# The adaLN product, the first load of x, the last store and the bias tables of the dilated heads rewritten

## The chip, the cores and the metric

One core of one Trainium2 chip runs the whole program. The metric is the device time of one execution in microseconds (us), as the median of several runs. Engines are written PE (matmul), PEld (weight load), DVE, ACT, POOL and SP; a "q" behind a name is the engine's DMA queue.

## What is computed

Two stacks of two layers over x of 256 rows and 1024 columns, all in fp32. A layer of the first stack is: SwiGLU feed-forward, a mixer of sliding-window attention and retention, a second feed-forward, each followed by a residual and a layer norm. A layer of the second stack is one mixer whose heads include six dilated heads, modulated by adaLN. What the change touches:

```python
def swiglu_ffn(x, w_gu, w_down):
    a, u = jnp.split(x @ w_gu, 2, axis=-1)
    return (jax.nn.silu(a) * u) @ w_down
...
# adaLN of a layer of the second stack: shift, scale and gate, 1024 each
mod = silu(c) @ w_ada + b_ada
# score bias of dilated head h between positions at distance dist
bias = log(count(dist)) - 2.0 ** (-8.0 * (h + 1) / 10.0) * dist
```

The bias's count says in how many of the dilation patterns (every key up to 128 back, every fourth, every sixteenth) a pair stands; pairs in none are masked.

## The kernel before, in words

**Weights.** All weights come in the order of one host-made list (`plan`) as pieces of up to 128 x 1024 fp32 (512 KB), loaded by SP's queue into `st`, a pool of 6 slots (NS). A product in fp32 is made of three: ACT rounds a piece to `whi` (line 300), DVE subtracts to get `wlo` (line 302), and PE multiplies hi by hi, hi by lo and lo by hi (`mm`, line 331). A slot is free again when DVE has read it, so an SP load waits, in order, for the DVE six slots back.

**Feed-forward.** `gu_T` (from line 520) makes one chunk of 128 gate and 128 up columns, transposed. For each of 8 steps k and two column halves it issues a pair of matmuls: one with `whi` against 512 columns (x hi and x lo side by side), one with `wlo` against 256. So a chunk has 16 pairs. There are 22 chunks; the down product `ac<-x..,h..` runs 6 chunks behind.

**Start.** The first feed-forward needs x transposed. `load_xT` (line 231) loads it in four quarters of 256 KB on SP's queue, each into one of the same six `st` slots, and splits it into `xx` (lines 377 and 378); the first chunk's weights come in pieces of 128, 128, 256, 256 and 256 KB (FIRST_K) between the quarters, the second chunk's as two of 512 KB. 18 bf16 matmuls on zeros go ahead on PE.

**adaLN.** `w_ada_2` is spread over the feed-forwards as pieces of 128 rows by 1024 columns, 48 in all (2 layers, 3 outputs, 8 row blocks). `ada_step` (line 306) multiplies each by its 128 values of silu(c) and adds it to `ada` on DVE (line 317, line 315 for the first of eight). After the eighth, eight transposes on PE (line 446) in two groups and two reductions on DVE (line 324) sum `ada` over the partitions into a column of `mod`. This happens six times, so 12 groups of four transposes.

**Dilated heads.** In each layer of the second stack, `score` makes the six dilated heads' scores in six banks: 384, 384, 512, 512, 256 and 256 columns. Line 660 adds the bias from `al`, which has two halves used in turn; line 1165 fills a half per bank, one DVE instruction per head, from `dist` and `lc` (log of the count). Then line 665 takes the row maximum, line 671 (ACT) the exponential, line 678 the reciprocal, line 1114 (ACT) the scaling, PE transposes P, and `PT` is copied by line 692 (ACT) or 694 (DVE) for the product with v (`ac<-PT,v..`). Beside it, ACT makes `sg` (line 1270), ahead of which its function table is loaded.

**Store.** The last layer norm writes each half of 128 rows in two scalings (line 422) and two stores on SP's queue (line 424).

The order of each engine's work is the order in which the code issues it, but for `issue_after`, which puts DVE and ACT work behind a named instruction.

Of the kernel before, what the change touches and what calls it, by code (L numbers as in the profile page):

```python
# [17 lines left out]
D = 1024  # L18
# [8 lines left out]
FIRST_K = ((0, 1), (1, 1), (2, 2), (4, 2), (6, 2))  # L27
# [31 lines left out]

G1 = in1_groups()  # L60
# [3 lines left out]
def plan(take):  # L64

    def piece(kind, name, l, k0, kk, cols):
        return kind, kk, len(cols), take(name, l, k0, kk, cols)

    def ffn(i, l):
        start = (i, l) == (1, 0)
        c0 = 0 if start else 4
        na = 0
        for c in range(0, c0, 2):
            cols = rng(128 * c, 256) + rng(DFF + 128 * c, 256)
            for k in (0, 2, 4, 6):
                yield piece("w", f"ffn{i}_w_gu", l, k, 2, cols)
        for c in range(c0, NCH):
            cols = rng(128 * c, 128) + rng(DFF + 128 * c, 128)  # L80
            for k, kk in FIRST_K if start and c == 0 else ((0, 4), (4, 4)):
                yield piece("w", f"ffn{i}_w_gu", l, k, kk, cols)
            if c >= NCH - 8 * len(ADA[i, l]):
                u, k = divmod(na, 8)
                al, q = ADA[i, l][u]
                yield piece("a", "w_ada_2", al, k, 1, rng(1024 * q, 1024))
# [12 lines left out]
    def outp(name, l):  # L99
        for k in range(8):  # L100
            yield piece("w", name, l, k, 1, rng(0, D))

    for l in range(DEPTH):
        yield from ffn(1, l)
        yield from groups("w_in", l, G1)
        yield from outp("w_out", l)
        yield from ffn(2, l)
    for l in range(DEPTH):
        yield from groups("w_in_2", l, G2[:5])
        for j in range(2):  # L110
            for k in (0, 3):
                yield piece("w", "w_uq_2", l, k, 3, rng(288 * j, 288))
        for k in range(2):
            yield piece("w", "w_ukv", l, k, 1, rng(0, 768))
        yield from groups("w_in_2", l, G2[5:])
        yield from outp("w_out_2", l)


def lay_out(inp):
    d = {}  # L120
    f = lambda a: np.ascontiguousarray(a)
    src = {**inp, "w_ukv": np.concatenate([inp["w_uk_2"], inp["w_uv_2"]], 2), "w_out_2": inp["w_out_2"][:, Y2]}
# [7 lines left out]
    d["xT"] = f(inp["x"][0].T.reshape(4, 2, 128, 2, 128).transpose(0, 2, 3, 1, 4).reshape(4, 128, 512))  # L130
    d["bada"] = f(inp["b_ada_2"].reshape(DEPTH * 24, 128).T)
    d["c"] = f(inp["c_2"].reshape(8, 128).T)
# [10 lines left out]
def tables():  # L143
# [31 lines left out]
    t["lc"] = lc.astype(f32)  # L175
    t["dist"] = dist.astype(f32)
    return {k: np.ascontiguousarray(v) for k, v in t.items()}
# [5 lines left out]
class Kernel:  # L183
# [12 lines left out]
    def setup(self):  # L196
# [9 lines left out]
        self.c = self.const.tile([128, 8], F32, name="c")  # L206
        self.sc = self.const.tile([128, 8], F32, name="sc")
        self.mod = [self.const.tile([128, 24], F32, name=f"mod{l}") for l in range(DEPTH)]
        nc.gpsimd.dma_start(out=self.idn, in_=d["idn"])
# [4 lines left out]
        nc.scalar.activation(out=self.sc, in_=self.mhalf, func=AF.Silu)  # L214
        self.xx = self.xt.tile([128, 2, 2, 8, 128], F32R, name="xx")
        self.xh, self.xl = self.xx[:, 0], self.xx[:, 1]
        self.xhl = self.xx.rearrange("p e t k n -> p (e t) k n")
        self.xT, self.yT = {}, {}
        self.n_ox = 0
        self.warm()  # L220
# [10 lines left out]
    def load_xT(self, q):  # L231

        st = self.stage.tile([128, 1024], F32, name="st")[:, :512]
        self.nc.sync.dma_start(out=st, in_=self.d["xT"][q])
        ks = slice(2 * q, 2 * q + 2)
        self.hilo(self.xh[:, :, ks, :], self.xl[:, :, ks, :], st.rearrange("p (t k n) -> p t k n", t=2, k=2))

    def load_x(self, c):

        if c == 7:  # L240
            for t in range(2):
                self.xT[t] = self.xh[:, t], self.xl[:, t]
                self.nc.sync.dma_start(out=self.x[t], in_=self.d["x"][128 * t:128 * t + 128, :])
            self.bada = self.const.tile([128, 48], F32, name="bada")
            self.nc.sync.dma_start(out=self.bada, in_=self.d["bada"])
            self.nc.sync.dma_start(out=self.c, in_=self.d["c"])
            self.nc.scalar.activation(out=self.sc, in_=self.c, func=AF.Silu)
# [6 lines left out]
    def open_block1(self):  # L254
# [5 lines left out]
        self.dec = p.tile([128, 2048], F32, name="dec")  # L260

# [3 lines left out]
    def open_block2(self):  # L265
# [6 lines left out]
        self.lc = p.tile([128, 384], F32, name="lc")  # L272
        for n in ("rt2", "cau", "dist", "lc"):
            nc.gpsimd.dma_start(out=getattr(self, n), in_=d[n])
# [31 lines left out]
    def ada_step(self, pool):  # L306

        nc = self.nc
        while self.pieces and self.pieces[0][0] == "a":
            _, l, k, _, cols = self.pieces[0][3]  # L310
            st = self.load_piece()[1]
            c = self.sc[:, k:k + 1]
# [5 lines left out]
            if k < 7:  # L318
                continue
            q = cols[0] // 1024  # L320
# [79 lines left out]
    def ln(self, t, banks, alpha, eps, gate=None):  # L400
# [16 lines left out]
        if self.at_end:  # L417
# [3 lines left out]
            for c0, c1 in HALVES:  # L421
                nc.vector.scalar_tensor_tensor(out=x[:, c0:c1], in0=x[:, c0:c1], scalar=y, in1=self.b[:, c0:c1],  # L422
                                               op0=ALU.mult, op1=ALU.add)
                nc.sync.dma_start(out=self.out[128 * t:128 * t + 128, c0:c1], in_=x[:, c0:c1])
# [50 lines left out]
class Ffn:  # L475
# [44 lines left out]
    def gu_T(self, c, pcs):  # L520
# [7 lines left out]
        for hi, lo, kk, _ in pcs:  # L528
            for i in range(kk):
                for j in range(2):  # L530
                    cs = slice(128 * j, 128 * j + 128)
                    o = ps[j].rearrange("p (a n) -> p a n", a=4)
                    K.mm(o, lhsT=hi[:, i, cs], rhs=K.xhl[:, :, k, :], start=k == 0, stop=False, skip_group_check=True)
                    K.mm(o[:, 0:2, :], lhsT=lo[:, i, cs], rhs=K.xh[:, :, k, :], start=False, stop=k == 7,
# [28 lines left out]
    def body(self):  # L563
        K = self.K
        if self.start:
            pcs = []
            for q in range(4):
                K.load_xT(q)
                pcs += K.get(1 if q else 2)
            self.gu_T(0, pcs)  # L570
        last = K.split
        for c in range(1 if self.start else 4, NCH):
            self.gu_T(c, K.get(2))
            if c in (7, 13, 15) and self.start:
                K.load_x(c)
            with K.tc.issue_after(last):
                K.ada_step(self.fp)
# [367 lines left out]
class Mixer2(OutProj, Attn):  # L945
# [223 lines left out]

    def body(self):  # L1170
# [128 lines left out]
        b_score, b_av = self.make(6, 0.125, half(qbT), keys(kbT), vb, 5, self.alibi(0, lambda t: self.seg(K.lc, t)), True)  # L1299
# [98 lines left out]
```

## Time and profile before

| | |
|---|---|
| median of 3 runs | 1345.4 us (1343.68, 1345.4, 1346.33) |
| the profiled execution | 1350.96 us, its span 1349.2 us |
| mean granted clock of TensorE | 0.994 |
| PE busy | 1319.8 us, 98% of the span |
| DVE busy / ACT busy / POOL busy | 76% / 55% / 2% |
| mean DMA rate | 195 GB/s |

The span is the time from the first to the last record; 1.8 us of the execution lie around it. In a timeline row the numbers are start and duration, both in us, then the engine, line, operation, output and inputs, shapes and count. A bracket at the end gives the idle time of the engine just before and what ended it. Matmuls overlap, so a matmul's duration is longer than the step from one to the next.

### The profile page before, as it was taken

How to read it: one execution, taken by the hardware profiler on the slowest of the kernel's cores; microseconds unless marked ns; L12 is line 12 of the kernel's file. 1: busy time of each engine (PE TensorE's matmuls, PEld its weight loads, DVE VectorE, ACT ScalarE, POOL GpSimd, SP SyncE). 2: the span in 40 equal slices, each digit the busy share in tenths (PEclk: the TensorE clock that was granted, in tenths of full speed). 3: DMA queues.
4: the chain of work that ended last, by engine and by line, in shares of the span. 5: the costliest groups of instructions: out<-in, count | busy, mean ns of one | idle time of the engine just before them, and what ended most of it. 6: DMA issues, size and time to landing. Idle time of an engine off the chain costs nothing. (4 is left out here: it accounts for less than half of the span.)

```text
span 1349.2 us, 20437 instructions
## 1 busy us (share of the span) xinstructions
PE 1319.8 (98%) x7654; PEld 1135.5 (84%) x7654; DVE 1031.4 (76%) x1713; ACT 741.4 (55%) x1310; POOL 25.8 (2%) x35
## 2 busy tenths in 40 slices
PE   8999999999999999999999999999999999999997
PEld 6888888788887888888887878888889998799886
DVE  6876769968977669787579878687585797866976
ACT  6654536446655546545446456555355678456681
POOL 0000000010000000000000110000000000000000
PEclk9999999999999999999999999999999999999999
DMA  8987724546878628877423637677445433464420
GB/s 290 332 297 234 240 93 133 203 134 232 316 244 268 212 83 305 299 255 250 156 96 125 252 124 269 202 260 265 131 151 184 154 126 128 138 203 160 143 77 32
DMA packets 75235, 262.88 MB, mean 195 GB/s; under 512 B 9168, under 2 KB 9552, under 8 KB 75008
## 3 DMA queue, kind: packets, MB, share of 16 engines
q1 hardware_dynamic: 74592, 259.82, 56.9%
q0 software_dynamic: 544, 1.75, 0.4%
q8 instruction: 60, 0.98, 0.3%
q14 instruction: 39, 0.32, 0.1%
HBM read 260.49 MB, written 1.05 MB: 194 GB/s over the span
## 5 line engine op out<-in xcount | busy, mean ns | idle before, releaser
L302 DVE TENSOR_TENSOR wlo<-st,whi 128x1024 fp32r<-128x1024 f32 (+4 forms) x319 | 372.3, 1176 | 74.6 <-ACT whi L300 73.1
L300 ACT ACTIVATE whi<-st 128x1024 fp32r<-128x1024 f32 (+4 forms) x319 | 322.6, 1021 | 123.4 <-PE mm L331 49.6
L331 PE MATMUL mm<-xx,whi 128*128 128x256 f32 (+1 forms) x1296 | 335.0, 334 | 1.2 <-DVE xx L378 1.2
L331 PE MATMUL mm<-xx,wlo 128*128 128x256 f32 x928 | 262.1, 283 | 0.0
L331 PEld LDWEIGHTS mm<-xx,whi 128*128 128x128 f32 x1296 | 221.0, 191 | 25.7 <-ACT whi L300 1.5
L331 PE MATMUL mm<-whi,xx 128*128 128x512 f32 (+3 forms) x744 | 219.1, 372 | 0.6 <-DVE xx L378 0.4
L331 PE MATMUL tr<-xx,whi 128*128 128x512 f32 x560 | 197.3, 394 | 2.2 <-ACT whi L300 2.2
L331 PEld LDWEIGHTS mm<-xx,wlo 128*128 128x128 f32 x928 | 176.8, 191 | 2.2 <-DVE wlo L302 0.5
L331 PE MATMUL tr<-xx,wlo 128*128 128x256 f32 x560 | 157.6, 282 | 0.5 <-DVE wlo L302 0.5
L331 PEld LDWEIGHTS mm<-whi,xx 128*128 128x128 f32 x744 | 135.0, 188 | 24.5 <-issue 1.6
L302 DVE TENSOR_TENSOR xlo<-st,xhi 128x1024 fp32r<-128x1024 f32 x106 | 128.4, 1219 | 26.0 <-ACT xhi L300 26.0
L300 ACT ACTIVATE xhi<-st 128x1024 fp32r<-128x1024 f32 x106 | 110.2, 1056 | 67.6 <-PE ac L331 56.3
L331 PE MATMUL mm<-wlo,xx 128*128 128x512 f32 (+3 forms) x372 | 137.0, 369 | 0.0
L331 PEld LDWEIGHTS tr<-xx,whi 128*128 128x128 f32 x560 | 105.4, 188 | 26.0 <-ACT whi L300 2.6
L331 PE MATMUL ac<-xlo,hth 128*128 128x512 f32 x320 | 126.2, 394 | 0.0
L331 PE MATMUL ac<-xhi,hth 128*128 128x512 f32 x320 | 125.4, 392 | 0.0
L331 PEld LDWEIGHTS tr<-xx,wlo 128*128 128x128 f32 x560 | 106.5, 190 | 2.2 <-DVE wlo L302 1.0
L331 PE MATMUL ac<-xhi,htl 128*128 128x512 f32 x320 | 105.0, 392 | 0.0
L317 DVE SCALAR_TENSOR_TENSOR ada<-st,sc,ada 128x1024 f32<-128x1024 f32 x42 | 53.8, 1281 | 41.5 <-DMA st<-in_w 41.5
L331 PEld LDWEIGHTS mm<-wlo,xx 128*128 128x128 f32 x372 | 70.1, 188 | 10.6 <-issue 0.3
L331 PEld LDWEIGHTS ac<-xhi,hth 128*128 128x128 f32 x320 | 60.1, 188 | 14.1
L331 PEld LDWEIGHTS ac<-xhi,htl 128*128 128x128 f32 x320 | 60.0, 188 | 12.4
(275 smaller groups left out, 1823.1 us busy)
## 6 DMA issues: line engine op xcount, KB each, us to landing
st<-in_w SPq DMA_DIRECT2D x442, 512.0 KB, 4.6
st<-in_w SPq DMA_DIRECT2D x20, 384.0 KB, 3.7
g<-in_lng SPq DMA_DIRECT2D x8, 512.0 KB, 4.8
b<-in_lnb SPq DMA_DIRECT2D x8, 512.0 KB, 5.2
st<-in_w SPq DMA_DIRECT2D x8, 432.0 KB, 4.1
st<-in_w SPq DMA_DIRECT2D x8, 296.0 KB, 3.9
st<-in_xT SPq DMA_DIRECT2D x4, 256.0 KB, 4.5
x<-in_x SPq DMA_DIRECT2D x2, 512.0 KB, 7.7
```

The source lines that it names most:

```text
L300: nc.scalar.activation(out=hi[:, :m], in_=st[:, :m], func=AF.Copy)
L302: nc.vector.tensor_tensor(out=lo[:, :m], in0=st[:, :m], in1=hi[:, :m].bitcast(F32), op=ALU.subtract)
L317: nc.vector.scalar_tensor_tensor(out=self.ada, in0=st, scalar=c, in1=self.ada, op0=ALU.mult, op1=ALU.add)
L331: return self.nc.tensor.matmul(*a, **k).ins
```

## The change

Four edits.

1. `w_ada_2` is transposed on the host, so a piece holds 128 output columns against all 1024 inputs. silu(c) is loaded onto all 128 partitions (512 KB, one ACT instruction of 128 x 1024). Each of the 48 pieces takes one DVE instruction that multiplies and sums along the row into its column of `mod`. The transposes and reductions are gone.
2. x's quarters are loaded into tiles that are idle at the start (`x[1]`, half of `x[0]`, `tmp`) and not into `st`; the first quarter comes as two DMAs on ACT's queue. `xx` has hi and lo of one k side by side. The second chunk's weights come as 256, 256 and 512 KB. `idn` and c are loaded later, at chunk 7.
3. The last store of 512 columns is split in 384 (ACT's queue) and 128.
4. The dilated heads' biases are made on the host, and each bank's half of `al` is loaded by POOL's queue. `lc` is not loaded.

```diff
-FIRST_K = ((0, 1), (1, 1), (2, 2), (4, 2), (6, 2))
+FIRST_K = (((0, 1), (1, 1), (2, 2), (4, 2), (6, 2)), ((0, 2), (2, 2), (4, 4)))
...
-        nc.scalar.activation(out=self.sc, in_=self.mhalf, func=AF.Silu)
...
+        self.xk = self.xt.tile([128, 8, 512], F32R, name="xx")
+        self.xh, self.xl = (self.xk[:, :, c:c + 256].rearrange("p k (t n) -> p t k n", t=2) for c in (0, 256))
...
+        self.xw = self.tmp()
+        for k in range(2):
+            nc.scalar.dma_start(out=self.x[1][:, 256 * k:256 * k + 256], in_=d["xT"][0][:, 256 * k:256 * k + 256])
+        nc.scalar.activation(out=self.one, in_=self.mhalf, func=AF.Silu)
...
+    def load_xT(self, k, n):
+        q, r = divmod(k, 2)
+        src = (self.x[1][:, 0:512], self.x[1][:, 512:], self.x[0][:, 512:], self.xw)[q][:, 256 * r:256 * (r + n)]
+        if q > 0:
+            self.nc.sync.dma_start(out=src, in_=self.d["xT"][q])
+        self.hilo(self.xk[:, k:k + n, :256], self.xk[:, k:k + n, 256:], src.rearrange("p (k n) -> p k n", k=n))
...
-            if k == 0:
-                self.ada = pool.tile([128, 1024], F32, tag="ada", name="ada", bufs=2)
-                nc.vector.tensor_scalar(out=self.ada, in0=st, scalar1=c, scalar2=None, op0=ALU.mult)
-            else:
-                nc.vector.scalar_tensor_tensor(out=self.ada, in0=st, scalar=c, in1=self.ada, op0=ALU.mult, op1=ALU.add)
...
+            nc.vector.scalar_tensor_tensor(out=st, in0=st, scalar=1.0, in1=self.sc, op0=ALU.mult, op1=ALU.mult,
+                                           accum_out=self.mod[l][:, j:j + 1])
...
-            for h in range(2):
-                ps = self.transposes([self.ada[:, 512 * h + 128 * i:512 * h + 128 * i + 128] for i in range(4)])
-                nc.vector.tensor_reduce(out=m[:, 4 * h:4 * h + 4], in_=ps.rearrange("p (k n) -> p k n", k=4), axis=AX.X,
-                                        op=ALU.add)
...
-            for c0, c1 in HALVES:
+            for c0, c1, q in ((0, 512, nc.sync), (512, 896, nc.scalar), (896, 1024, nc.sync)):
...
+    def alibi_b(self, t, hs, nk):
+        self.n_al += 1
+        w = self.al[:, self.n_al % 2, :len(hs) * nk]
+        self.K.nc.gpsimd.dma_start(out=w, in_=self.K.d[f"al{B_BANKS.index((nk, tuple(hs)))}"])
+        return w.rearrange("p (h n) -> p h n", h=len(hs))
...
-        b_score, b_av = self.make(6, 0.125, half(qbT), keys(kbT), vb, 5, self.alibi(0, lambda t: self.seg(K.lc, t)), True)
+        b_score, b_av = self.make(6, 0.125, half(qbT), keys(kbT), vb, 5, self.alibi_b, True)
```

**Order at the start, SP's queue.** Before, with what each load waits for (`st<-in_xT` is a quarter of x, `st<-in_w` a piece of weights; DVE is the slot's last reader):

```order
L234 DMA st<-in_xT 128x512
L284 DMA st<-in_w 128x256 x2
L234 DMA st<-in_xT 128x512
L284 DMA st<-in_w 128x512
L234 DMA st<-in_xT 128x512
L284 DMA st<-in_w 128x512 [waits DMAHW0_49,DVE_49]
L234 DMA st<-in_xT 128x512 [waits DMAHW1_49,DVE_49]
L284 DMA st<-in_w 128x512 [waits DMAHW2_49,DVE_49]
L284 DMA st<-in_w 128x1024 [waits DMAHW3_49,DVE_49]
L284 DMA st<-in_w 128x1024 [waits DMAHW4_49,DVE_49]
```

And now (`x_80`, `x_79` and `tmp` are the idle tiles):

```order
L290 DMA st<-in_w 128x256 x2
L240 DMA x_80<-in_xT 128x512
L290 DMA st<-in_w 128x512
L240 DMA x_79<-in_xT 128x512
L290 DMA st<-in_w 128x512
L240 DMA tmp<-in_xT 128x512 [waits DMAHW0_49]
L290 DMA st<-in_w 128x512 [waits DMAHW1_49]
L290 DMA st<-in_w 128x512 [waits DMAHW2_49]
L290 DMA st<-in_w 128x512 [waits DMAHW3_49,DVE_49]
L290 DMA st<-in_w 128x1024 [waits DMAHW4_49,DVE_49]
```

The first load that waits for DVE is now the tenth, the second piece of chunk 1; it was the seventh, and chunk 1's first piece stood behind four such waits.

**Order around a group of transposes on PE.** Before, at the end of a feed-forward (`hth` and `htl` are the chunk's hidden values):

```order
L331 MATMUL ac<-xhi,hth 128x512
L446 MATMUL tr<-idn,ada 128x128 x4
L331 MATMUL ac<-xlo,hth 128x512
L331 MATMUL ac<-xhi,htl 128x512 x2
L331 MATMUL ac<-xhi,hth 128x512
L446 MATMUL tr<-idn,ada 128x128 x4
L331 MATMUL ac<-xlo,hth 128x512
```

In the changed kernel the two rows of transposes are gone and nothing stands in their place; the rows around them are the same.

**Order at the first two banks of the dilated heads on DVE.** Now, with the waits (`P<-ac,al` is line 660 before; DMASW is a load of POOL's queue):

```order
L657 SCALAR_TENSOR_TENSOR P<-ac,al 128x512 [waits DVE_49,PE_49] x2
L662 TENSOR_REDUCE nm<-P 128x2 [waits DVE_49] x2
L308 TENSOR_TENSOR kkw<-st,qiTw 128x1024 [waits DMAHW7_49,Activation_49]
L675 RECIPROCAL rd<-den 128x2 [waits Activation_49]
L657 SCALAR_TENSOR_TENSOR P<-ac,al 128x384 [waits DMASW4_49,PE_49]
L675 RECIPROCAL rd<-den 128x2 [waits Activation_49]
L657 SCALAR_TENSOR_TENSOR P<-ac,al 128x384 [waits DMASW5_49,PE_49]
L662 TENSOR_REDUCE nm<-P 128x3 [waits DVE_49] x2
L691 COPY PT<-tr 128x512 [waits PE_49]
```

On POOL, the loads that these wait for:

```order
L1171 DMA al<-in_al 128x384 x2
L1171 DMA al<-in_al 128x512 x2
L1171 DMA al<-in_al 128x256 x2
```

Before, DVE's `al<-dist,lc` stood where `kkw` stands, and again between the banks; each load on POOL waits until DVE has read the same half two banks earlier.

## Rows read from the trace of the kernel before

**Rows 1.** The page's section 1: busy us, share of the span, instructions.

```profile
PE 1319.8 (98%) x7654; PEld 1135.5 (84%) x7654; DVE 1031.4 (76%) x1713; ACT 741.4 (55%) x1310; POOL 25.8 (2%) x35
```

**Rows 2.** The waits of PE: us in total, times, longest.

```profile
PE tr L446 <- DVE sa L541: 3.3, 2, 2.0
PE tr L446 <- ACT qT L764: 2.0, 1, 2.0
PE ac L331 <- ACT y L1042: 2.0, 2, 1.5
```

**Rows 3.** The timeline of PE from chunk 1 (`tr`) to chunk 3 (`tr`).

```profile
15.16 0.73 PE L331 MATMUL tr<-xx,whi 128*128 128x512 f32 x2 [2.25 <-ACT whi L300]
16.42 0.80 PE L331 MATMUL tr<-xx,wlo 128*128 128x256 f32 x2 [0.53 <-DVE wlo L302]
...
23.16 0.40 PE L331 MATMUL mm<-xx,whi 128*128 128x512 f32 x1
...
28.81 0.40 PE L331 MATMUL tr<-xx,whi 128*128 128x512 f32 x1
```

**Rows 4.** Window: PE, PEld, DVE, ACT, POOL busy (count); PEclk, DMA, GB/s.

```profile
16.00:18.00 2.00, 1.58 (x5) 1.47 (x6) 2.00 (x4) 1.87 (x3) 0.00 (x0) 0.57 1.03 420
```

**Rows 5.** The timelines of SP, ACT and DVE at chunk 1's first loads.

```profile
8.19 0.33 SPq L284 DMA_DIRECT2D st<-in_w  x1
...
10.29 0.63 ACT L300 ACTIVATE whi<-st 128x512 fp32r<-128x512 f32 x1
14.05 1.06 ACT L300 ACTIVATE whi<-st 128x1024 fp32r<-128x1024 f32 x1 [3.12 <-DMA st<-in_w]
...
15.13 1.23 DVE L302 TENSOR_TENSOR wlo<-st,whi 128x1024 fp32r<-128x1024 f32 x1 [3.49 <-ACT whi L300]
```

**Rows 6.** The timeline of PE at two groups of transposes.

```profile
409.48 0.65 PE L446 MATMUL tr<-idn,ada 128*128 128x128 f32 x4 [2.03 <-DVE sa L541]
...
410.21 0.39 PE L331 MATMUL ac<-xhi,hth 128*128 128x512 f32 x1
410.43 0.39 PE L331 MATMUL ac<-xlo,hth 128*128 128x512 f32 x1
```

**Rows 7.** Groups of instructions: count, busy us, mean ns, idle time before.

```profile
L317 DVE SCALAR_TENSOR_TENSOR ada<-st,sc,ada 128x1024 f32<-128x1024 f32 x42 | 53.8, 1281 | 41.5 <-DMA st<-in_w 41.5
...
L324 DVE TENSOR_REDUCE mod<-tr 128x4 f32<-128x512 f32 x12 | 8.2, 687 | 2.7 <-PE tr L446 2.7
```

**Rows 8.** The timeline of DVE at the first layer's dilated heads.

```profile
1106.13 1.28 DVE L660 SCALAR_TENSOR_TENSOR P<-ac,al 128x512 f32<-128x512 f32 x2
...
1108.51 0.88 DVE L1165 SCALAR_TENSOR_TENSOR al<-dist,lc 128x128 f32<-128x128 f32 x4
...
1109.39 0.53 DVE L660 SCALAR_TENSOR_TENSOR P<-ac,al 128x384 f32<-128x384 f32 x1
...
1122.05 1.28 DVE L660 SCALAR_TENSOR_TENSOR P<-ac,al 128x512 f32<-128x512 f32 x2
```

**Rows 9.** The timelines of ACT and PE behind them.

```profile
1113.93 0.97 ACT L1114 ACTIVATE P<-P,rd 128x128 f32<-128x128 f32 x3
1114.92 1.28 ACT L1270 ACT_TABLE_LOAD   x1
...
1117.59 0.58 ACT L692 ACTIVATE PT<-tr 128x512 f32<-128x512 f32 x1
...
1118.54 0.66 PE L331 MATMUL ac<-PT,vc 128*64 128x128 f32 x8
...
1122.79 0.88 PE L331 MATMUL ac<-PT,vbt 128*64 128x128 f32 x12 [0.38 <-DVE P L660]
```

**Rows 10.** DMA issues: count, KB each, median us from issue to landing.

```profile
out_x<-x SPq DMA_DIRECT2D x4, 256.0 KB, 2.1
...
cau<-in_cau POOLq DMA_DIRECT2D x1, 192.0 KB, 3.8
...
bada<-in_bada SPq DMA_DIRECT2D x1, 24.0 KB, 7.8
```

More of the change, by code (lines that the diff above doesn't have):

```diff
@@ L80, in ffn @@
             cols = rng(128 * c, 128) + rng(DFF + 128 * c, 128)
-            for k, kk in FIRST_K if start and c == 0 else ((0, 4), (4, 4)):
+            for k, kk in FIRST_K[c] if start and c < 2 else ((0, 4), (4, 4)):
                 yield piece("w", f"ffn{i}_w_gu", l, k, kk, cols)
@@ L85, in ffn @@
                 al, q = ADA[i, l][u]
-                yield piece("a", "w_ada_2", al, k, 1, rng(1024 * q, 1024))
+                yield piece("a", "w_ada_T", al, 8 * q + k, 1, rng(0, 1024))
                 na += 1
@@ L121, in lay_out @@
     f = lambda a: np.ascontiguousarray(a)
[L122 removed]
+    src = {**inp, "w_ukv": np.concatenate([inp["w_uk_2"], inp["w_uv_2"]], 2), "w_out_2": inp["w_out_2"][:, Y2],
+           "w_ada_T": inp["w_ada_2"].transpose(0, 2, 1)}
     def take(name, l, k0, kk, cols):
@@ L174, in tables @@
     lc = np.where(cnt > 0, np.log(np.maximum(cnt, 1.0)), NEG)
-    t["lc"] = lc.astype(f32)
     t["dist"] = dist.astype(f32)
+    for n, (k, heads) in enumerate(B_BANKS):
+        c = slice(0, 128) if k == 128 else slice(128, 384)
+        t[f"al{n}"] = np.concatenate([lc[:, c] - 2.0 ** (-8.0 * (h + 1) / 10.0) * dist[:, c] for h in heads], 1).astype(f32)
     return {k: np.ascontiguousarray(v) for k, v in t.items()}
@@ L205, in setup @@
         self.idn = self.const.tile([128, 128], F32, name="idn")
-        self.c = self.const.tile([128, 8], F32, name="c")
-        self.sc = self.const.tile([128, 8], F32, name="sc")
+        self.one = self.const.tile([128, 8], F32, name="one")
         self.mod = [self.const.tile([128, 24], F32, name=f"mod{l}") for l in range(DEPTH)]
-        nc.gpsimd.dma_start(out=self.idn, in_=d["idn"])
         self.gc = self.const.tile([128, 64], F32, name="gc")
@@ L245, in load_x @@
             self.nc.sync.dma_start(out=self.bada, in_=self.d["bada"])
-            self.nc.sync.dma_start(out=self.c, in_=self.d["c"])
-            self.nc.scalar.activation(out=self.sc, in_=self.c, func=AF.Silu)
+            self.nc.sync.dma_start(out=self.idn, in_=self.d["idn"])
+            self.nc.sync.dma_start(out=self.sc, in_=self.d["c"].to_broadcast([128, D]))
+            self.nc.scalar.activation(out=self.sc, in_=self.sc, func=AF.Silu)
         for n in {7: (), 13: ("gc", "bc", "rt1", "win"), 15: ("dec",)}[c]:
@@ L260, in open_block1 @@
         self.dec = p.tile([128, 2048], F32, name="dec")
+        self.sc = p.tile([128, D], F32, name="sc")
     def close_block1(self):
@@ L271, in open_block2 @@
         self.dist = p.tile([128, 384], F32, name="dist")
-        self.lc = p.tile([128, 384], F32, name="lc")
-        for n in ("rt2", "cau", "dist", "lc"):
+        for n in ("rt2", "cau", "dist"):
             nc.gpsimd.dma_start(out=getattr(self, n), in_=d[n])
@@ L531, in gu_T @@
                     cs = slice(128 * j, 128 * j + 128)
-                    o = ps[j].rearrange("p (a n) -> p a n", a=4)
-                    K.mm(o, lhsT=hi[:, i, cs], rhs=K.xhl[:, :, k, :], start=k == 0, stop=False, skip_group_check=True)
-                    K.mm(o[:, 0:2, :], lhsT=lo[:, i, cs], rhs=K.xh[:, :, k, :], start=False, stop=k == 7,
+                    K.mm(ps[j], lhsT=hi[:, i, cs], rhs=K.xk[:, k, :], start=k == 0, stop=False, skip_group_check=True)
+                    K.mm(ps[j][:, :256], lhsT=lo[:, i, cs], rhs=K.xk[:, k, :256], start=False, stop=k == 7,
                          skip_group_check=True)
@@ L566, in body @@
             pcs = []
-            for q in range(4):
-                K.load_xT(q)
-                pcs += K.get(1 if q else 2)
+            for k, n in FIRST_K[0]:
+                K.load_xT(k, n)
+                pcs += K.get(1)
             self.gu_T(0, pcs)
@@ L572, in body @@
         for c in range(1 if self.start else 4, NCH):
-            self.gu_T(c, K.get(2))
+            self.gu_T(c, K.get(3 if self.start and c == 1 else 2))
             if c in (7, 13, 15) and self.start:
@@ L576, in body @@
             with K.tc.issue_after(last):
-                K.ada_step(self.fp)
+                K.ada_step()
             if c == 11:
```

24 lines of the change are left out of this document (8 added, 16 removed).

## The prediction

> **What bounds the kernel.** I read the page's busy shares first: PE is busy for 98% of the span, DVE for 76%, ACT for 55% [rows 1]. So time is won by taking work off PE, by closing a gap in it, or by ending the work behind it sooner; taking work off DVE or ACT wins nothing unless PE waits for it. The second view is the list of what PE waits for [rows 2]: its waits are few and short, and two of them, 3.3 us together, stand in front of the transposes of `ada`. Third I read the timeline at the four places that the change touches.
>
> **Start: -4.8 us.** Chunk 1 begins on PE at 15.16, after 2.25 us without work, so chunk 0 ended at 12.91 [rows 3]. Chunk 2 begins at 23.16 and chunk 3 at 28.81, so a whole chunk takes 5.65 us and chunk 1 took 8.00. Of the 2.35 us more, 0.53 is a second wait, for `wlo`; the other 1.8 goes with a granted clock of 0.57 in the two microseconds after the gap [rows 4], part of which was at 1.2 GHz in place of 2.4. The gap ends with `whi` of chunk 1's first piece. That piece was issued at 8.19, since it stood behind four loads that waited for a slot of `st`, and ACT got it at 14.05: 5.9 us after issue [rows 5]. Now x takes none of the six slots, and the order on SP shows one piece more with a slot of its own. Without the waits the earlier loads leave SP every 0.4 us or so, which puts this piece's issue near 4.4. From there the transfers bound it, not the issue. At 420 GB/s [rows 4] 256 KB take 0.65 us, so I put its landing 0.65 after ACT took chunk 0's last piece at 10.29 [rows 5], that is at 10.9. ACT and DVE take about 0.6 each for half of the 1.06 and 1.23 that a full piece takes, so `wlo` is there at 12.3, before chunk 0 ends. The last 512 KB land 0.65 + 1.3 later, at 12.9, and are split at 15.2; PE needs them after eight of 16 pairs, at 12.75 + 2.8 = 15.6. So chunk 1 would run from 12.75 through at full clock and end at 18.4, not 23.16. If the transfers are only as late as to leave half of the gap and the half clock, it is -2.5; if chunk 0 too ends earlier because its `xx` comes in smaller steps, -6.0.
>
> Here one rule speaks against the edit. The Trainium skill, "DMA: Bandwidth & Descriptors", section "Issuing engines are not separate DMA queues", says that loads issued from several engines share the same 16 DMA engines, and that this saves only the time of the issuing. By that rule moving x's first quarter to ACT's queue gives less than a microsecond. The sum above doesn't rest on the queue but on the slots; the rule is the first rival.
>
> **xx side by side: 0.** PE reads the same columns in the same number of matmuls, now contiguous. No row of before has the contiguous form for this product, so 0, with 1 us either way: the steady step of 5.65 for 16 pairs is all matmul.
>
> **adaLN: -9.3 us.** Twelve groups of transposes leave PE. The first shown takes PE from 409.48 to 410.21, with one product in it of 0.22 (the step from 410.21 to 410.43): 0.51 for four transposes [rows 6]. Twelve times 0.5 is 6.0. The two waits ahead of them, 3.3, go as well [rows 2], since what stands next on PE needs nothing that was just made. Bounds: -6.0 if the two waits come back as waits for something else, -9.5 with 0.2 for shorter ones.
> DVE: removed are 42 instructions of 1281 ns, 12 of 687 [rows 7] and six shorter ones; added are 48 of the same shape with a sum. At 1281 ns these are 61.5 us against 62.0, so DVE is even. The sum along the row may cost more. The nearest extreme is a second pass of the same length, 2.56 in place of 1.28 for each piece, while DVE has a quarter of its time free [rows 1]: a chunk takes 5.65 on PE, its down product of 12 matmuls some 2.7 at the step of 0.22 [rows 6], so of 8.3 about 2 us are free, and 1.3 more per piece fit. I take 0, and 2 us as the bound above. The load of c, now 512 KB, and its one ACT instruction lie around chunk 7, beside PE's work, well before the first `ada` piece.
>
> A second rule bears on that. The Trainium skill, "Vector Engine (DVE) Microarchitecture Reference", section "Points that are easy to get wrong", says that this instruction with two non-bf16 sources in SBUF runs at half throughput, as both read ports are taken and none is left for reading back an accumulator. The old form has two such sources too, and its 1281 ns [rows 7] hold whatever that costs; no run here shows the form with an accumulator. If the time doubled again, the sum would not change, by the free 2 us above.
>
> **Store: -0.2 us.** The last stores leave one queue one after the other and 256 KB need 2.1 us to land [rows 10]; the last is now half as wide. Between 0 and -0.4.
>
> **Tables: +2.4 us.** Per layer 12 small instructions leave DVE, where they cost little (four take 0.88, [rows 8]); PE didn't wait for them. In their place banks wait for POOL's loads. The first load may be issued when DVE has read its half, about 1106.8, half way into the pair at 1106.13 [rows 8]; 192 KB on this queue took 3.8 us [rows 10], so it lands at 1110.65. The second is at 1111.3. The two `P<-ac,al` stood at 1109.39 and some 1.7 later: the first comes 1.3 late, and in the new order the pair's reductions stand behind both. The two sets of exponentials and scalings (0.97 per set of three) now go ahead of ACT's table load at 1114.92, where the second set had stood behind it; the load's 1.28, `sg`, and the copy `PT` at 1117.59 move on by about 2 us [rows 9]. PE's product with it stood at 1118.54, 0.4 after the copy's end; so PE idles some 1.3 to 1.7. The third and fourth banks' tables have until 1122.05, ten microseconds: hidden. The last two are issued after that and cost perhaps 0.3. The wait of 0.38 ahead of `ac<-PT,vbt` is absorbed, -0.4. So +1.2 per layer, +2.4 for two. Bounds: -0.8, if the loads are as quick as the 2.1 us of the stores [rows 10] and DVE gains; +10, if each stall also costs a lost clock of 1.8 us as at the start, in two places per layer.
>
> **The sum.** -4.8 - 9.3 - 0.2 + 2.4 = -11.9. The profiled execution took 1350.96, 5.6 over the median of the runs, so it would be 1339.1; on the median of 1345.4 it is 1333.5.
>
> **Rivals.**
> *The start is bound by the transfers* (the rule on queues): then chunk 1 begins as late as before but for one issue or two, -1.5 for -4.8, and the time is 1336.8. For it: the DMA engines moved 420 GB/s just then, at a share of 1.03 [rows 4]. Against: the piece was issued late, and landed when everything queued before it was through. 0.17.
> *The tables' stalls let the clock fall.* Four times 1.8 more, so -4.7 and 1340.7. For it: the fall after the gap of 2.25. Against: the stall I compute is shorter. 0.13.
> *Waits elsewhere close as well.* The waits of 2.0 for `qT` and 1.5 for `y` [rows 2] come from pieces that arrive late. If the shift of the stream of loads mends both, with 1.5 of clock each, -6.5 more: 1327. Nothing in the change touches them but the timing. 0.10.
> *The gain doesn't come*: the transposes' gaps return as other waits, and chunk 1 as in the first rival: -5.3, 1340. 0.03.
> *Slower.* POOL's loads are short but land in the middle of a stream of 512 KB pieces; `bada`, 24 KB in such a stream, took 7.8 us [rows 10], against 3.8 for `cau`. At 7.8 the first bank is at 1114.7, 5.3 late, and the last two banks, issued after 1123, some 4 late: with the clock 1.8 lost, 11 per layer, 22 in all, against the 14.3 gained elsewhere: 1353. It decides when a layer loses over 7, that is with landings over 9 us at one place or near 7.8 at both. Against: 7.8 was behind other loads on SP's own queue; on POOL's nothing stands ahead. 0.02.
> That the edits don't do what they say has the remaining 0.01, at no change.
>
> **The numbers.** The forecast has 0.54. Its own range, by the bounds of the start and of the adaLN, is 1330 to 1338. With the first two rivals and the third's edge the range is 1327 to 1341.5. A measurement can tell about 0.2%, 2.7 us. Faster by more: 0.93, since only the last two cases and the tables' worst bound lie above 1342.7; same 0.04; slower 0.03.
>
> **What would show it.** Chunk 2 of the first feed-forward should begin on PE near 18.4, with no half clock at 16 to 18. No `tr<-idn,ada` on PE, and PE busy down by about 6. The sum on DVE near 1.28. At the dilated heads: `al<-in_al` landings near 3.8 and one PE wait of 1 to 2 us per layer. The forecast is wrong if chunk 1 still waits for a DMA, if a piece of `ada` makes DVE late for `wlo`, or if POOL's loads need over 6 us.

## The result and the profile after

The changed kernel takes 1333.57 us (1333.35 to 1333.69, 4 runs), beside it the kernel before 1345.87: a ratio of 0.9911, with a 95% interval of 0.9894 to 0.9928. Forecast was 1333.5. On another chip it was 1333.72 against 1344.97, a ratio of 0.9924 (0.9908 to 0.994). The total came out as forecast; of the four terms in it three did not, as far as the runs below show.

The profiled execution took 1333.35, with a span of 1331.6. Its busy times, and what PE waits for (columns as in [rows 1] and [rows 2]):

```profile
PE 1306.7 (98%) x7606; PEld 1127.2 (85%) x7606; DVE 1018.0 (76%) x1729; ACT 742.7 (56%) x1312; POOL 31.2 (2%) x45
```

```profile
PE tr L444 <- ACT P L1111: 3.2, 4, 1.5
...
PE ac L329 <- ACT y L1039: 0.7, 1, 0.7
...
PE tr L444 <- ACT qT L761: 0.2, 1, 0.2
```

The 3.3 us ahead of the transposes of `ada` are gone [rows 2]. The waits for `qT` and `y`, which the change doesn't touch, are shorter here. In their place stands a wait of 3.2 for the scaling of P, in the stage of the dilated heads.

**Start.** The timeline of PE at the first three changes of chunk:

```profile
12.39 0.40 PE L329 MATMUL tr<-xx,whi 128*128 128x512 f32 x1
...
18.00 0.40 PE L329 MATMUL mm<-xx,whi 128*128 128x512 f32 x1
...
23.55 0.40 PE L329 MATMUL tr<-xx,whi 128*128 128x512 f32 x1
```

and the window that answers to [rows 4], with the same columns:

```profile
16.00:18.00 2.00, 2.00 (x13) 1.74 (x12) 2.00 (x3) 1.06 (x2) 0.00 (x0) 1.00 1.03 416
```

Chunk 1 runs without a gap and at the full granted clock. Chunk 2 begins at 18.00, not at 23.16 [rows 3]; 18.4 was forecast. ACT takes chunk 1's first two pieces straight after chunk 0's last, three in a row:

```profile
9.81 1.97 ACT L306 ACTIVATE whi<-st 128x512 fp32r<-128x512 f32 x3
```

**adaLN.** The groups of DVE that answer to [rows 7]: the multiply, and the reading of its sum, which the profile shows as an instruction of its own.

```profile
L318 DVE SCALAR_TENSOR_TENSOR st<-st,sc 128x1024 f32<-128x1024 f32 x48 | 58.6, 1222 | 47.7 <-DMA st<-in_w 47.7
...
L318 DVE DVE_READ_ACCUMULATOR st<-st,sc 128x1 f32 x48 | 3.9, 82 | 0.0
```

A piece takes 1.22 + 0.08 = 1.30 us, against 1.28 before [rows 7]. On PE no transposes stand among the down products any more: where a group stood at 409.48, behind a wait of 2.03 [rows 6], the products follow one another.

```profile
399.84 0.63 PE L329 MATMUL ac<-xhi,htl 128*128 128x512 f32 x2
400.30 0.40 PE L329 MATMUL ac<-xhi,hth 128*128 128x512 f32 x1
400.54 0.39 PE L329 MATMUL ac<-xlo,hth 128*128 128x512 f32 x1
```

**Tables.** The loads land about as fast as `cau` in [rows 10]:

```profile
al<-in_al POOLq DMA_DIRECT2D x4, 256.0 KB, 2.9
al<-in_al POOLq DMA_DIRECT2D x4, 192.0 KB, 4.1
...
al<-in_al POOLq DMA_DIRECT2D x4, 128.0 KB, 3.0
```

The wait they make is in the first layer's timeline, here from POOL, DVE, ACT and PE, which answers to [rows 8] and [rows 9]:

```profile
1088.81 1.12 POOL L1171 DMA_DIRECT2D al<-in_al  x2 [92.53 <-DVE P L657]
...
1093.16 0.56 DVE L657 SCALAR_TENSOR_TENSOR P<-ac,al 128x384 f32<-128x384 f32 x1 [1.92 <-DMA al<-in_al]
1093.63 0.15 DVE L675 RECIPROCAL rd<-den 128x2 f32<-128x2 f32 x1
...
1093.82 0.91 ACT L1111 ACTIVATE P<-P,rd 128x256 f32<-128x256 f32 x2 [1.47 <-DVE rd L675]
...
1092.01 0.84 PE L444 MATMUL tr<-idn,P 128*128 128x128 f32 x4 [0.34 <-ACT P L1111]
1094.38 0.44 PE L444 MATMUL tr<-idn,P 128*128 128x128 f32 x2 [1.54 <-ACT P L1111]
```

Read from the top: the first bank's load is issued at 1088.81, when DVE has read its half. DVE stands idle for 1.92 until it has landed. Behind the waiting add stands a reciprocal (1093.63) which has nothing to do with the table: it belongs to the heads scored before. ACT waits 1.47 for it, to scale P of those heads; PE waits 1.54 for that, to transpose P. One late load thus stops three engines in turn, by way of an instruction that only stands behind it.

### The profile page after: what moved, and what is told of

Its sections match the earlier page's. It is cut to its first block, busy times and chain, and to the rows that moved or that the text cites. A ratio compares the mean times of both kernels' runs of the same rounds, so it can differ in the third digit from the quotient of the medians.

```text
span 1331.6 us, 20391 instructions
## 1 busy us (share of the span) xinstructions
PE 1306.7 (98%) x7606; PEld 1127.2 (85%) x7606; DVE 1018.0 (76%) x1729; ACT 742.7 (56%) x1312; POOL 31.2 (2%) x45
## 4 chain that ended last, share of the span: by engine, by line
PE 76%; DVE 12%; DMA 4%; issue 3%; ACT 3%; POOL 1%; SPq 0%; DVEq 0%; POOLq 0%; ACTq 0%
PE mm L329 33%; PE ac L329 25%; PE tr L329 15%; DVE wlo L308 3%; PE tr L444 3%; DMA st<-in_w 2%; DMA al<-in_al 1%; POOL rs_y L387 1%; DVE P L657 1%; DVE acc L1072 1%; DVE xlo L308 1%; ACT P L668 1%; ACT P L1111 1%; DVE acc L1067 1%; DVE x L409 1%
## 5 line engine op out<-in xcount | busy, mean ns | idle before, releaser
L308 DVE TENSOR_TENSOR wlo<-st,whi 128x1024 fp32r<-128x1024 f32 (+5 forms) x320 | 372.4, 1174 | 71.5 <-ACT whi L306 68.4
L306 ACT ACTIVATE whi<-st 128x1024 fp32r<-128x1024 f32 (+5 forms) x320 | 322.9, 1018 | 119.3 <-PE mm L329 47.0
L318 DVE SCALAR_TENSOR_TENSOR st<-st,sc 128x1024 f32<-128x1024 f32 x48 | 58.6, 1222 | 47.7 <-DMA st<-in_w 47.7
```

What stands on the lines that cost most here:

```text
L306: nc.scalar.activation(out=hi[:, :m], in_=st[:, :m], func=AF.Copy)
L308: nc.vector.tensor_tensor(out=lo[:, :m], in0=st[:, :m], in1=hi[:, :m].bitcast(F32), op=ALU.subtract)
L318: nc.vector.scalar_tensor_tensor(out=st, in0=st, scalar=1.0, in1=self.sc, op0=ALU.mult, op1=ALU.mult, accum_out=self.mod[l][:, j:j + 1])
```

## The experiments

Where no chip is named, runs of one group shared the runs of the kernel before, whose median on that chip stands at the group's head. Differences are taken between medians. The changed kernel itself ran on the chip of the result and in the third group, not in the first two; there no. 3, which turned out equal to it, stands for it on the first group's chip.

**First group (before: 1343.16).** No. 1, the biases computed again:

```diff
...
-        for n in ("rt2", "cau", "dist"):
+        self.lc = p.tile([128, 384], F32, name="lc")
+        for n in ("rt2", "cau", "dist", "lc"):
...
-        b_score, b_av = self.make(6, 0.125, half(qbT), keys(kbT), vb, 5, self.alibi_b, True)
+        b_score, b_av = self.make(6, 0.125, half(qbT), keys(kbT), vb, 5, self.alibi(0, lambda t: self.seg(K.lc, t)), True)
```

> The changed kernel, but with the biases of the dilated heads computed on DVE as before. Theory: the loaded tables cost 3.8 us, 2.3 in the first of the two layers and 1.5 in the second, as PE's transposes of P wait for a reciprocal on DVE that stands behind the add that waits for the table. Then it takes 1333.6 - 3.8 = 1329.8 us (1329 to 1330.8) and PE's waits for the scaling of P, 3.2 us in the changed kernel, fall under 0.5. Rival: the table's wait only took the place of other waits of this stage, and computing puts them back: 1332.6 to 1334.6.

Measured: 1329.31 (1329.14 to 1329.54), 4.3 less than the changed kernel (4.2 less than no. 3, on one chip with it) and 0.9891 (0.9877 to 0.9904) of the kernel before. No wait for the scaling of P is left among those of PE. The theory holds, and this is the version that beats both kernels.

No. 2, three parts of `al` in turn (a small tile makes room for the third):

```diff
...
-        self.al = self.keep.tile([128, 2, 512], F32, tag="cl0", name="al")
+        self.al = self.keep.tile([128, 3, 512], F32, tag="cl0", name="al")
...
-        w = self.al[:, self.n_al % 2, :len(hs) * nk]
+        w = self.al[:, self.n_al % 3, :len(hs) * nk]
```

> The changed kernel with three parts of al used in turn, not two, so that the first bank's load waits for a reader three banks back, which is long done; the second bank's load is issued when the first's was. Theory: it is the time of issue of the first load, not the load, that costs: the first bank waits no longer, the reciprocal behind it comes at once, and 2.5 to 3.8 us of the 3.8 come back: 1329.8 to 1331.1. Rival: the loads themselves are slow or disturb the stream of weights, and then it stays at 1333 to 1334.

Measured: 1331.72 (1330.67 to 1332.34), 1.9 less than the changed kernel: under half of the 4.3. It lies outside both expectations, nearer to the theory's. DVE and PE in its first layer:

```profile
1089.56 0.55 DVE L656 SCALAR_TENSOR_TENSOR P<-ac,al 128x384 f32<-128x384 f32 x1
1091.16 0.21 DVE L674 RECIPROCAL rd<-den 128x2 f32<-128x2 f32 x2
1092.46 0.56 DVE L656 SCALAR_TENSOR_TENSOR P<-ac,al 128x384 f32<-128x384 f32 x1 [0.64 <-DMA al<-in_al]
```

```profile
1091.91 0.44 PE L443 MATMUL tr<-idn,P 128*128 128x128 f32 x2 [0.22 <-ACT P L1110]
```

The first bank doesn't wait, the reciprocals come ahead of the bank that does (the second, 0.64), and PE's wait at the transposes is 0.22 in place of 1.54. So the time of issue did cost the larger part of that wait. The same product of PE behind the first layer's heads, in the changed kernel, in no. 2 and in no. 1:

```profile
1130.53 0.50 PE L329 MATMUL ac<-xlo,xx 128*128 128x512 f32 x1 [0.53 <-DVE xlo L308]
...
1128.33 0.50 PE L328 MATMUL ac<-xlo,xx 128*128 128x512 f32 x1 [0.76 <-DVE xlo L307]
...
1127.67 0.50 PE L331 MATMUL ac<-xlo,xx 128*128 128x512 f32 x1 [0.21 <-DVE xlo L310]
```

At the first product with qbT the three stand level (1086.60 to 1086.63). So in these profiles the loaded tables cost 2.9 in the first layer, of which the third part brings back 2.2, and by the spans (1331.6, 1328.9 and 1327.4) 4.2 in both layers, of which it brings back 2.7. That the rest comes from the second bank's wait and the ones behind it is an inference; no run takes it apart.

No. 3, the last store in one piece:

```diff
-            for c0, c1, q in ((0, 512, nc.sync), (512, 896, nc.scalar), (896, 1024, nc.sync)):
+            for c0, c1, q in ((0, 512, nc.sync), (512, 1024, nc.sync)):
```

> The changed kernel with the last 512 columns scaled and stored in one piece as before. Theory from the tails of the two traces: the split makes the tail behind PE's last matmul 0.3 us longer (8.38 against 8.08), so it takes 1333.3 and its tail is 8.1. Rival, as the prediction had it: the split saves 0.2, so it takes 1333.8 and the tail is 8.6.

Measured: 1333.55, no difference, and a tail of 8.36 behind PE's last matmul, as with the split (8.38). Neither expectation holds: the split is worth nothing either way. Its profiled execution took 1337.30, and shows what the tables can do. PE's wait in the first dilated layer, and a window behind it:

```profile
1095.52 0.69 PE L444 MATMUL tr<-idn,P 128*128 128x128 f32 x2 [1.68 <-ACT P L1111]
```

```profile
1096.00:1098.00 2.00, 2.00 (x11) 2.00 (x11) 2.00 (x4) 2.00 (x11) 0.23 (x1) 0.50 0.80 244
```

The wait is 1.68 where the changed kernel had 1.54, and here the granted clock is 0.50 behind it, 1.2 GHz in place of 2.4. The second rival of the prediction happens, but only in some executions. The other four runs of no. 3 took 1332.68 to 1334.15. The slowest load of a table took 5.0 in this one, 4.3 in the changed kernel's.

No. 4, the old adaLN in the changed kernel: `ada_step`, the layout of `w_ada_2` and the load of c as before.

```diff
-                yield piece("a", "w_ada_T", al, 8 * q + k, 1, rng(0, 1024))
+                yield piece("a", "w_ada_2", al, k, 1, rng(1024 * q, 1024))
...
-            nc.vector.scalar_tensor_tensor(out=st, in0=st, scalar=1.0, in1=self.sc, op0=ALU.mult, op1=ALU.mult,
-                                           accum_out=self.mod[l][:, j:j + 1])
+            if k == 0:
+                self.ada = pool.tile([128, 1024], F32, tag="ada", name="ada", bufs=2)
+                nc.vector.tensor_scalar(out=self.ada, in0=st, scalar1=c, scalar2=None, op0=ALU.mult)
...
```

> The changed kernel with the adaLN as before: weights not transposed, sums over partitions by transposes on PE. Theory: the transposes and the waits ahead of them cost PE 10.2 us, so it takes 1343.8 (1342.5 to 1345). Rival: only the work of the transposes counts, twelve times 0.5, since the waits ahead of them are from this one profiled execution: 1339.6 (1338.8 to 1340.5).

Measured: 1344.83, 11.3 more than the changed kernel; 1.0012 (1.0002 to 1.0022) of the kernel before. The theory holds, and the waits ahead of the transposes are no accident of one execution; in this run they are

```profile
PE tr L452 <- DVE sa L546: 3.8, 2, 2.4
```

What a group costs where PE doesn't wait for it, and the clock behind the longer of the two waits:

```profile
170.88 0.40 PE L337 MATMUL ac<-xhi,hth 128*128 128x512 f32 x1
171.21 0.66 PE L452 MATMUL tr<-idn,ada 128*128 128x128 f32 x4
171.63 0.47 PE L337 MATMUL ac<-xlo,hth 128*128 128x512 f32 x1
```

```profile
404.00:408.00 4.00, 3.96 (x15) 3.32 (x16) 2.45 (x5) 0.84 (x2) 0.00 (x0) 0.57 0.98 351
```

From one product to the next it is 0.75 with a group between, 0.23 without: 0.5 for a group, as forecast. Behind the wait of 2.4 the granted clock is 0.57 over four microseconds, mostly 1.2 GHz. So the new adaLN alone carries the gain of the whole change; what the start wins the tables take.

**Second group (before: 1344.01).** The parts of the start, one at a time. No. 5, x's first quarter on SP's queue:

```diff
-            nc.scalar.dma_start(out=self.x[1][:, 256 * k:256 * k + 256], in_=d["xT"][0][:, 256 * k:256 * k + 256])
+            nc.sync.dma_start(out=self.x[1][:, 256 * k:256 * k + 256], in_=d["xT"][0][:, 256 * k:256 * k + 256])
```

> The changed kernel with x's first quarter on SP's queue again, ahead of the first weights, still in an idle tile. Theory: chunk 1 needs an early issue of its first piece, which the free slots give; two issues of 0.43 us more on SP make everything behind them 0.9 later at most, so chunk 2 of the first feed-forward begins at 18.0 to 18.9 and it takes 1333.6 to 1334.5. Rival: the gain of the start comes from the second queue; then chunk 2 begins after 20 and it takes 1336 or more.

No. 6, that and x in slots of `st`:

```diff
-        self.xw = self.tmp()
+        self.xs = {0: self.stage.tile([128, 1024], F32, name="st")}
...
+        if q not in self.xs:
+            self.xs[q] = self.stage.tile([128, 1024], F32, name="st")
+            self.nc.sync.dma_start(out=self.xs[q][:, :512], in_=self.d["xT"][q])
+        src = self.xs[q][:, 256 * r:256 * (r + n)]
```

> As the run with x's first quarter on SP's queue, and x's quarters in slots of st again; chunk 1 still comes in pieces of 256, 256 and 512 KB. Theory: the slots decide. The sixth load waits for DVE again, chunk 1's first piece is issued near 7 to 8 and not near 4.5, the gap ahead of chunk 1 returns with 1 to 2.3 us and, if it is as long as before, the clock falls: chunk 2 begins at 19.5 to 23, the time is 1335 to 1338.5. Rival: the transfers bound the start, whatever the time of issue: chunk 2 begins within 0.5 of the run with x's first quarter on SP's queue.

No. 7, chunk 1 in two pieces of 512 KB:

```diff
-FIRST_K = (((0, 1), (1, 1), (2, 2), (4, 2), (6, 2)), ((0, 2), (2, 2), (4, 4)))
+FIRST_K = (((0, 1), (1, 1), (2, 2), (4, 2), (6, 2)), ((0, 4), (4, 4)))
...
```

> The changed kernel with chunk 1's weights in two pieces of 512 KB as before. Theory: a piece of 512 KB lands about 0.65 us later than one of 256 KB and ACT and DVE take 0.5 each longer for it, so wlo of chunk 1's first piece is ready some 1.7 later than the 11.4 of the changed kernel, at 13.1, where chunk 1 began at 12.39: a gap of 0.7, the time 1334 to 1334.6. Rival: the small pieces carry most of the gain of the start: a gap of 2 and a low clock, 1337 or more.

No. 8, the kernel before, no edit:

> The kernel before once more, for a second profile. Theory: of the 17.6 us between the two profiled executions 6.1 are of waits of the first one that come and go with the landing of single loads, ahead of the transposes of rk at 708 (2.0 and the low clock behind it) and of the product at 1284 (1.5 and the low clock): this profile lacks at least one of them and takes 1343 to 1348. Rival: these waits belong to the kernel, and the change mends them: both are there again, with over 1.4 us each.

**Third group (before: 1344.97).** No. 9, the changed kernel, no edit, 1333.72:

> The changed kernel once more, beside the kernel before on one chip. Theory, from the second profile of the kernel before (1343.25, chunk 2 of the first feed-forward at 20.2): the gain is 2.3 at the start and some 10.5 for the adaLN, less 3.5 for the tables, so 9 to 11 of the median of before (1334 against 1344). Rival: the sum of the prediction, with the start at 4.8: 11.5 to 13.

No. 10, the edits of nos. 6 and 7 together. It is nearly the start as before: x's first quarter still comes as two loads, `idn` is still loaded at chunk 7 and not at 1.25 on POOL's queue, and hi and lo of x stay side by side.

> The changed kernel with the whole start as before: x's quarters in slots of st and on SP's queue, chunk 1 in two pieces of 512 KB; hi and lo of x stay side by side. Theory from the second profile of the kernel before: chunk 2 begins at 19.5 to 21 and it costs 1.5 to 3 us against the changed kernel, with a spread between runs of 1.6 or more, as the landing of chunk 1's first piece moved from 14.05 to 12.44 between two profiles of the kernel before, issued at the same time. Rival, the prediction's 4.8: chunk 2 near 23 and 4 to 5.5 us.

No. 11, the kernel before once more, no edit:

> The kernel before a third time, for its profile. Theory: the wait ahead of chunk 1 lies anywhere between 0.3 and 2.3 us, as one load lands; the waits ahead of the transposes of rk and the product with qbT come and go. The waits ahead of the transposes of ada stay, 3 to 4 us in two places. Rival: the start's wait is 2 or more in most runs and the second profile was the odd one.

What these seven measured, with the begin of chunks 1 and 2 on PE in the profiled execution:

| kernel | chunk 1 | chunk 2 | median us |
|---|---|---|---|
| changed, first profile / no. 9 | 12.39 / 12.31 | 18.00 / 17.90 | 1333.57 / 1333.72 |
| no. 5, first quarter on SP | 13.14 | 18.73 | 1335.31 |
| no. 6, and x in slots | 12.49 | 19.09 | 1334.90 |
| no. 7, chunk 1 in 512 KB | 12.22 | 18.61 | 1334.20 |
| no. 10, nos. 6 and 7 together | 13.16 | 19.70 | 1336.24 |
| before, first profile | 15.16 | 23.16 | 1345.87 |
| before, no. 8 / no. 11 | 13.55 / 14.79 | 20.08 / 22.71 | 1344.01 / 1344.97 |

By the medians, against no. 9, nos. 5, 6 and 7 lose 1.6, 1.2 and 0.5, and no. 10 loses 2.5. The runs of one kernel lie further apart than that (no. 9: 1332.77 to 1337.14; no. 10: 1335.28 to 1338.69), and nos. 5 to 7 ran on another chip than no. 9, so the medians don't rank the parts. By chunk 2's begin, which two profiles of the changed kernel have within 0.1, they lose 0.7 to 0.8, 1.1 to 1.2, 0.6 to 0.7, and no. 10 1.7 to 1.8. No part decides. No. 5 agrees with its theory by chunk 2's begin and is above it by the median. No. 6 lies below its theory: with x in slots chunk 1's first piece is issued at 6.84,

```profile
6.84 1.48 SPq L291 DMA_DIRECT2D st<-in_w  x2
...
9.94 1.29 ACT L307 ACTIVATE whi<-st 128x512 fp32r<-128x512 f32 x2
```

over two microseconds later than in the changed kernel (4.49), yet ACT takes that piece straight behind chunk 0's last (two in a row at 9.94), and chunk 1 begins at 12.49, without a gap; the cost comes 3 us later, from its third piece. So the time of issue alone doesn't set when the first piece is used. Chunk 2 begins within 0.4 of no. 5's, as the rival says; that the transfers bind it is the rival's reading, and no run shows it by itself. No. 7 agrees with the theory: a gap of 0.45, for `wlo` at 13.32, where 0.7 was expected. No. 10 agrees with the theory (19.70, and 2.5 us), against the 4.8 of the prediction; but in it ACT takes x's second quarter at 5.49, and in three profiles of the kernel before at 6.68 to 6.81, so what it leaves out of the old start may count too.

No. 8 took 1343.25 in its profiled execution, and has neither the wait of 2.0 for `qT` nor its low clock, as its theory said. It shows too that the gap ahead of chunk 1 is not always there. PE and ACT in it:

```profile
13.55 0.73 PE L331 MATMUL tr<-xx,whi 128*128 128x512 f32 x2 [0.49 <-ACT whi L300]
14.81 0.50 PE L331 MATMUL tr<-xx,wlo 128*128 128x256 f32 x2 [0.53 <-DVE wlo L302]
```

```profile
12.44 1.06 ACT L300 ACTIVATE whi<-st 128x1024 fp32r<-128x1024 f32 x1 [1.52 <-DMA st<-in_w]
```

The same load, issued at 8.06 in place of 8.19, is there at 12.44 in place of 14.05 [rows 5]. The gap is 0.49 and the clock stays at 1.00 (a window of 13 to 17 us). In no. 11 the gap is 1.91, with a clock of 0.50 behind it:

```profile
14.79 0.73 PE L331 MATMUL tr<-xx,whi 128*128 128x512 f32 x2 [1.91 <-ACT whi L300]
```

```profile
16.00:18.00 2.00, 1.95 (x7) 1.75 (x8) 2.00 (x4) 1.60 (x3) 0.00 (x0) 0.50 1.03 420
```

As its theory said, the gap moves (2.25, 0.49 and 1.91 in the three profiles, in order), while the waits ahead of the transposes of `ada` stay: 3.3, 3.7 and 3.9. Its rival, that a gap near 2 is the usual case and no. 8 the odd one, is not excluded by three profiles. No. 9's theory put the gain at 9 to 11; it was 11.2, just over that and just under its rival's 11.5. It doesn't tell them apart; no. 10 speaks for the theory, within the limits said.

No. 12, in the third group, does each multiply of the adaLN twice:

```diff
+            nc.vector.scalar_tensor_tensor(out=st, in0=st, scalar=1.0, in1=self.sc, op0=ALU.mult, op1=ALU.mult,
+                                           accum_out=self.one[:, 0:1])
```

> The changed kernel with the multiply-and-sum of each of the 48 pieces of w_ada done twice (the second into a column that nobody reads): 48 x 1.31 = 63 us more on DVE. Theory, the prediction's: DVE has about 2 us free in a chunk with such a piece, so PE's end moves by less than 1 us, 1333 to 1335. Rival: the pieces and the splits of the weights stand in one queue on DVE, and wlo comes late where it is just in time now: 0.2 us or more per piece, 1343 or more.

Measured: 1333.90, 0.2 more than no. 9, whose runs lie between 1332.77 and 1337.14. The theory holds. DVE has 62 us of instructions more (50 of busy time, since they overlap), and the time doesn't show them:

```profile
L320 DVE SCALAR_TENSOR_TENSOR st<-st,sc 128x1024 f32<-128x1024 f32 x48 | 58.5, 1218 | 0.0
...
L320 DVE DVE_READ_ACCUMULATOR st<-st,sc 128x1 f32 x48 | 4.0, 83 | 0.0
```

## Why the prediction was right, and where it was not

| term | predicted | measured, by which run |
|---|---|---|
| start | -4.8 | -2.5 (no. 10 against no. 9; not quite the whole start) |
| adaLN | -9.3 | -11.3 (no. 4) |
| store | -0.2 | 0.0 (no. 3) |
| tables | +2.4 | +4.3 (no. 1) |
| sum | -11.9 | -9.5 |
| the whole change | -11.9 | -12.3, and -11.2 on another chip |

**Start: right in the trace, its size taken from one execution.** Chunk 2 was forecast at 18.4 and began at 18.00 and 17.90. The kernel before has it at 23.16, 20.08 and 22.71, so the gain was 5.2, 2.1 or 4.7, as one takes the profile; the medians of no. 10 say 2.5. What failed is the step that took the gap of 2.25 and the low clock behind it as the kernel's own: no. 8 has a gap of 0.49 and no low clock. How often the long gap comes isn't known, so the term's mean isn't either. The prediction noted that this execution was 5.6 above the median, but subtracted from it as if the excess lay elsewhere. Between the spans of this profile and of no. 8 (1349.2 and 1341.5) lie 7.7, of which 3.1 are there when chunk 2 begins; the waits for `qT` and `y`, which no. 8 has not or shorter, are among the rest. A second step is weaker than it was put: the slots do make the issue late (8.19), but no. 6 shows that an issue over two microseconds later hardly moves the use of the first piece. The first rival, 0.17, may have part of the mechanism. The rule of its page, "DMA: Bandwidth & Descriptors" of the Trainium skill, section "Issuing engines are not separate DMA queues", that a second issuing engine saves only the time of the issuing, agrees with the trace of no. 5: the second queue brings chunk 2 forward by 0.7 us (18.73 to 18.00), somewhat under the two issues of 0.43 that it saves. A slip without effect: chunk 0 ends at 12.91 in the prediction's reading and at 12.75 in its sum.

**adaLN: right, too small.** The groups of transposes go, and the waits with them. A group costs 0.5, as forecast (0.75 - 0.23 in no. 4), so twelve cost 6.2; the two waits are 3.8 there, where 3.3 was taken. These make 10.0. What the term put at nothing is the clock behind those waits: the first profile and no. 8 have none low there, but no. 4 has 0.57 over four microseconds, which costs some 1.7 (an estimate: 0.43 of 4), and no. 11 a stretch of 0.50 behind its wait of 2.12. With it no. 4's profile comes to 11.7, beside 11.3 by the medians. PE's busy time fell by 13.1 and not by 6, but three stretches at a low clock stand in the first profile; against no. 8, which has none, it fell by 8.7. The step on DVE held: 1.30 per piece, and with as much again nothing changes (no. 12). The rule of the Trainium skill, "Vector Engine (DVE) Microarchitecture Reference", section "Points that are easy to get wrong", that such an instruction runs at half throughput as no port is left to read an accumulator back, doesn't show as a doubling here: with an accumulator the form takes 1222 ns and 82 for the reading, without it 1281 [rows 7]. Whether both run at half of some other rate, no run shows.

**Store: 0.** The tail is the same.

**Tables: the sign right, the size short, and the place another.** The load's time was right (4.1 for 192 KB, 3.8 taken), and so was what becomes of ACT's order: all six scalings of P go ahead of ACT's table load, which in no. 1 stands at 1095.73 with three ahead of it. ACT and PE in the changed kernel, then PE in no. 1:

```profile
1097.06 1.85 ACT L1111 ACTIVATE P<-P,rd 128x128 f32<-128x128 f32 x6
1098.93 1.28 ACT L1274 ACT_TABLE_LOAD   x1
...
1100.72 0.66 PE L329 MATMUL ac<-PT,vc 128*64 128x128 f32 x8
...
1098.50 0.66 PE L331 MATMUL ac<-PT,vc 128*64 128x128 f32 x8
```

The step that failed is "so PE idles some 1.3 to 1.7", put at the product with `PT`. PE comes there 2.2 late, and doesn't wait: it has lost its time before, at the transposes of P of other heads, whose reciprocal stands on DVE behind the waiting add. Nor is the wait ahead of `ac<-PT,vbt` absorbed, for which 0.4 was taken off: it is 0.39 in the changed kernel too (at 1105.83). The prediction asked what becomes of the waiting instruction's result, and not what stands behind it on its engine. Per layer 1.2 was forecast; by the profiles it is 2.9 in the first and 1.3 in the second. The second rival, a low clock behind this stall, is not in the median but in single executions: of nine profiles with tables in two parts, those of nos. 3, 6 and 12 have it (1337.30, 1337.12 and 1334.06), no. 6 behind a wait of 2.48 and a load of 5.5.

**xx side by side: 0, as forecast.** A chunk without waits takes 5.54 to 5.66 in profiles of the old layout (nos. 11 and 8) and 5.55 to 5.66 in those of the new.

The errors of the start and the store (+2.5), of the adaLN (-2.0) and of the tables (+1.9) come to +2.4, so the terms sum to -9.5. That the forecast's total was hit to 0.1 is luck: errors of about 2 in three terms, of both signs, and a median of the kernel before that is the highest of four.

The whole change gave -12.3 and -11.2 where it was measured itself. On the first group's chip no. 3, which is the changed kernel but for a store that costs nothing, takes 9.6 less than the kernel before (1333.55 against 1343.16). There the sum of the terms, -9.5, agrees with the whole, if the start's 2.5, which is from another chip, holds there too. The 2 to 3 us between the chips are in the kernel before, whose median lay between 1343.16 and 1345.87 and whose runs scatter from 1340.28 to 1347.77, while the three medians of the changed kernel and of no. 3 lie between 1333.55 and 1333.72. Its start, with a gap of 0.49 to 2.25, is one place where it scatters; whether the chip matters, no run tells.

## What to carry to other kernels

- A gap in one profile may belong to that execution. Where the profiled execution lies above the median by about as much as the gap that one means to close, a second profile comes first.
- When an edit makes an instruction wait, list what stands behind it on the same engine and who waits for that. Here an independent reciprocal behind a waiting add stopped PE, where the prediction had followed only the loaded table's own results.
- A transfer that replaces cheap work on an engine off the critical path needs its buffer free early. The computed tables were 4.3 us faster than the loaded ones, at 6 us more of busy time on DVE.

## What was not expected of the hardware

The granted clock falls behind some idle stretches of PE and not behind others of the same length. A wait of 1.54 ahead of the product with qbT was followed by 0.51 in the kernel before:

```profile
1286.00:1289.00 3.00, 3.00 (x15) 3.00 (x15) 3.00 (x13) 3.00 (x13) 0.00 (x0) 0.51 0.39 142
```

A wait of 1.54 in the changed kernel, shown above at 1094.38, was followed by 1.00, and so was the one of 2.03 ahead of the transposes of `ada` [rows 6]:

```profile
1095.00:1097.00 2.00, 2.00 (x19) 2.00 (x18) 1.98 (x4) 2.00 (x12) 0.08 (x1) 1.00 0.81 262
```

```profile
409.50:412.00 2.50, 2.50 (x15) 2.18 (x16) 2.50 (x5) 0.52 (x2) 0.00 (x0) 1.00 0.80 267
```

And a shorter wait, of 1.36 in no. 12, was followed by 0.50:

```profile
1093.53 0.69 PE L446 MATMUL tr<-idn,P 128*128 128x128 f32 x2 [1.36 <-ACT P L1113]
```

```profile
1094.00:1096.00 2.00, 2.00 (x12) 2.00 (x11) 2.00 (x4) 2.00 (x11) 0.23 (x1) 0.50 0.81 244
```

So the length of the wait alone doesn't decide; what does, no run here tells. And the time of one load moves more than was thought: the same 512 KB at the start took 5.9 us from issue to use in one profile and 4.4 in another.
